# A two-block transformer on one core: the order of the 64x64 F32 products in its two recurrent branches

## The chip, the cores and the metric

The kernel runs on one core of a Trainium2 chip. The time is the device time of one execution in microseconds (us); lower is better. Five engines work side by side, each on its own queue in order: TensorE (PE in the profile; PEld is its weight load, PEq its sequencer), VectorE (DVE), ScalarE (ACT), GpSimdE (POOL) and SyncE (SP), which here only issues transfers. TensorE is an array of 128 by 128 cells. A product whose stationary operand has 64 rows and 64 columns takes one quarter of it: the row half is the half of the 128 partitions that both operands lie on, the column half is the half of the partitions of PSUM, the accumulators, that the result goes to. TensorE's clock has two levels, 2.4 and 1.2 GHz; the profile gives the granted clock as 1.00 and 0.50.

## What is computed

The reference runs 512 tokens of 1024 channels through a first block (differential attention beside a pooling branch, then a mixture of 32 experts) and a second block of two layers. The change lies in the second block. Each of its layers projects the normed input and runs three branches: a gated delta rule (6 heads, "GDN"), latent attention (6 heads, "MLA"), and a second delta rule with its own decays (4 heads, "RWKV"). Both delta rules run over chunks of 64 tokens, forward and backward at once. The part that matters, for the first of them:

```python
def step(s, inp):
    w_c, u0_c, p_c, qg_c, kd_c, ge_c = inp
    u = u0_c - jnp.einsum('nhcd,nhde->nhce', w_c, s)
    o = jnp.einsum('nhcd,nhde->nhce', qg_c, s) + jnp.einsum('nhij,nhje->nhie', p_c, u)
    s = ge_c[..., None, None] * s + jnp.einsum('nhcd,nhce->nhde', kd_c, u)
    return s, o
_, o = lax.scan(step, s0, xs)
```

A head's state `s` is 64x64, and so are the chunk's matrices: every product in a step is 64x64 by 64x64. All is F32.

## The kernel before

Heads come in pairs, one on partitions 0 to 63, the other on 64 to 127 (`par` is the half, `half(i)` its slice). Tokens come in tiles of 128, a tile holding two chunks (`c` is the half). `d` is the direction; at step `st` the forward direction works on chunk `st` and the backward one on chunk `7 - st`, which lie on opposite halves. So `par`, `c` and `d` decide on which quarter of the array a product lies; the pair of heads (`hp` of three in GDN, `cp` of two in RWKV) doesn't.

`Gdn.chain` is the first branch's recurrence. Each of its 8 steps has three blocks of 12 products with vector work between them:
- `kp<-SA,kq`: the state read with k, on all four quarters; VectorE then scales it and subtracts it from v (`rhs`).
- `pu<-rhs,LT`: the chunk's solve, a product with the inverse triangle. Rows and columns are the chunk's half, so only two quarters, the diagonal ones, are used, one for each direction.
- `kp<-VS,KD`: what is added to the state, on all four quarters; VectorE adds it (`SA`). The last step has none.

After the steps come the outputs, for four tiles of tokens: 24 products of the states with q (`kp<-SA,kq`) and 24 of the inner part (`pu<-VS,LT`, diagonal quarters, two directions summed in PSUM), with one buffer each.

`Rwkv.states` has the same shape with 8 products in a block: `kp<-ST,KR`, then `pu<-rhs,LT`, then the state block of 16, where each result is the sum of two products (`kp<-vt,BK` and `kp<-AKV,BK`); then outputs, 16 products `pu<-AKV,RB` and 16 `kp<-ST,KR` a tile. Ahead of it, `products` in `Rwkv.prepare` multiplies a tile's scores with v: 16 products `mm<-vt,SC` on diagonal quarters, for four tiles and two directions.

The order on TensorE is the order in which the program is written. `Net.weave` braids several generators: each yields after some products the time that its next ones wait for other engines, and products of another generator fill that time. GDN's steps are braided with the input projection (`mm<-hh,wh` and its kin, 128x128 by 128x512), RWKV's `prepare` and `states` with MLA and the output projection. These products between two blocks are called fillers below. `Net.matmul` (line 145) issues all products, so they share a line and are told apart by the names of their tiles. The other engines' order is set by the framework's scheduler. An F32 product is recorded as two weight loads and two matmuls, so a block of 12 products shows as 24.

Of the kernel before, what the change touches and what calls it, by code (L numbers as in the profile page):

```python
# [17 lines left out]
S = 512  # L18
# [15 lines left out]
def const_arrays():  # L34
    """Arrays that depend on shapes alone."""
# [32 lines left out]
    # transposed: x -> (-x[16:32], x[0:16]) in each 32  # L68
# [4 lines left out]
    # window / count of the pooling windows that the ends cut  # L73
# [17 lines left out]
def half(p):  # L91
    return slice(64 * p, 64 * p + 64)
# [9 lines left out]

def mm3(net, out, a, b, start, stop):
    """out (+)= a.T @ b for a, b in two float32r parts each."""
    net.matmul(out, a[0], b[0], start=start, stop=False)
    net.matmul(out, a[0], b[1], start=False, stop=False)
    net.matmul(out, a[1], b[0], start=False, stop=stop)


class Net:  # L110
    """What the parts of the kernel share."""

    def __init__(self, ctx, tc, cst, xstack):
# [33 lines left out]
    def warm(self, psum, n):  # L147
        """Products that nobody reads: the tensor engine's clock is halved after an idle time."""
# [57 lines left out]
class Front:  # L206
    """The first block up to its second norm."""

    def __init__(self, net, ctx, ring, a):
# [16 lines left out]
        # normed x, then q and k, then x, by halves of the columns; x after the branch in two float32r parts takes the  # L226
        # place of these and of v and the pooling branch
# [13 lines left out]
    def loads(self, first):  # L241
        """The small inputs: those for the first norm, and the others."""
# [32 lines left out]
    def ada_rows(self, w):  # L275
        """512 columns of silu(c) @ w_ada, as four partial sums, on partitions 0, 32, 64, 96."""
# [10 lines left out]
    def ada_channels(self, i, ws):  # L287
        """mod[i]: a shift and a scale by channel p * 8 + k, and the norm's weight times 1 + scale."""
# [15 lines left out]
    def ada_gates(self):  # L304
        """The gates' rows, on every partition."""
# [22 lines left out]
    def normed(self):  # L328
        """rms_norm(x) by channel, without weights."""
# [16 lines left out]
    def scaled(self):  # L346
        """h = rms_norm(x) * (1 + sc1) + sh1 in two parts."""
# [9 lines left out]
    def in_load(self, i):  # L357
        """Columns 512 i .. of w_in, in halves; the first two lie where the pooling branch and v come later."""
# [10 lines left out]
    def parts(self, w, lo="vector"):  # L369
        """256 columns of w in two parts: a pair by k."""  # L370
# [10 lines left out]
    def by_token(self, i, w, dst, scale=1.0):  # L381
        """Columns 512 i .. of h @ w_in."""
# [10 lines left out]
    def rotary(self, i):  # L393
        """The rotary embedding of the first 16 dims of each component, and channels to partitions."""
# [23 lines left out]
    def pooled(self, w):  # L418
        """The pooling branch, by channel."""
# [38 lines left out]
    def attention(self):  # L458
# [4 lines left out]
        def scores(t, h):  # L463
# [11 lines left out]
            # e0 - lam * (s0 / s1) * e1, for s0 times the weights  # L475
# [35 lines left out]
    def heads(self, t, po, sums):  # L511
        """The normed heads of a tile of tokens, by channel."""
# [24 lines left out]
    def out(self, ws):  # L537
        """x += g1 * (mix @ w_out)."""
# [16 lines left out]
    def router(self):  # L555
        """The router's logits, from x before its norm, and the norm's factors; x in two parts."""
# [3 lines left out]
        # the weights with channels k * 128 + p  # L560
# [63 lines left out]
        # in memory that the parts of x take next: these come first  # L624
# [10 lines left out]
    def out_load(self, i):  # L635
        """Columns 256 i .. of w_out."""
# [58 lines left out]
class Ring:  # L695
    """Tiles of two pools in turn, n[0] of the first, then n[1] of the second."""
# [10 lines left out]
def experts_weights(net, rings, a, pr):  # L707
    """Weights of experts 2 * pr and 2 * pr + 1; pr may be a register."""
# [9 lines left out]
    # by halves of the channels, so that the next ones come as soon as half is done  # L718
# [7 lines left out]
    # by columns for w_down, so that little is left to do after the last  # L726
# [7 lines left out]
class Moe:  # L734
    def __init__(self, net, ctx, rings, a, xd):
# [25 lines left out]
    def route(self):  # L761
# [42 lines left out]
        # 1 + rank, and 0 for the others  # L804
# [15 lines left out]
        # the weights of two experts, and the factor of the norm, in two parts  # L820
# [7 lines left out]
        # the largest rank, for the tokens beyond an expert's first block  # L828
# [9 lines left out]
    def gather(self, rk2, wt2, block=0):  # L838
        """Tokens of ranks block * CAP .. of two experts, by channel; and what their outputs need."""
# [57 lines left out]
    def turned(self, pg, pu):  # L897
        """silu(gate) * up, by channel."""
# [42 lines left out]
    def experts(self, meanwhile):  # L941
        """The first CAP tokens of every expert, by pairs; some other work in between."""
# [27 lines left out]
    def overflow(self):  # L970
        """Experts with more than CAP tokens: the tokens beyond."""
# [26 lines left out]
    def squares(self, t):  # L998
        """x to DRAM; sums for rms_norm(x) * final_g and for the norm after it."""
# [1537 lines left out]
```

## Time and profile before

| | |
|---|---|
| median of three runs | 1983.79 us (1980.91 to 1987.42) |
| span of the profiled execution, first to last instruction | 1989.2 us (no other time of it is given) |
| TensorE matmuls busy | 1766.2 us, 89% of the span |
| VectorE busy | 1064.9 us, 54% |
| ScalarE, GpSimdE busy | 574.7 us, 548.0 us |
| GDN's steps and outputs, first and second layer | from 1038.6 to 1133.5 us and from 1608.9 to 1694.7 us |
| RWKV's states and outputs, first and second layer | from 1289.0 to 1372.4 us and from 1865.6 to 1949.4 us |

Busy time counts a stretch once, however many matmuls are in it, so matmuls that run beside each other on different quarters show as a shorter block and not as a higher share.

### The profile page before, as it was taken

Reading aid. Unit: us, or ns where it says so; the run is one execution under the profiler, and the core shown is the slowest. Engines: PE = TensorE matmul, PEld = TensorE weight load, DVE = VectorE, ACT = ScalarE, POOL = GpSimd, SP = SyncE. Lnnn points to the kernel's source line nnn. Section 1 sums busy time; section 2 is a strip of 40 time slices with the busy share of each in tenths; the row PEclk is TensorE's granted clock in tenths of the full one; section 3 lists DMA queues with packets and bytes.
Section 4 is the critical chain, followed back from the end, with each engine's and each line's share of the span. In section 5 each row is a group of like instructions: output and inputs, shape, how many; then the busy total and the mean of one; then the engine's idle time right before and its main releaser. Section 6 shows DMA issues by size and latency. Waiting matters only on the chain.

```text
span 1989.2 us, 34102 instructions
## 1 busy us (share of the span) xinstructions
PE 1766.2 (89%) x14010; PEld 1207.4 (61%) x14010; DVE 1064.9 (54%) x2260; ACT 574.7 (29%) x1134; POOL 548.0 (28%) x559
## 2 busy tenths in 40 slices
PE   5999998999999999696889988879886989898887
PEld 3985684444444444375677746657674878466566
DVE  2445434434343333568874467636678853756337
ACT  4354432121221212353230144411442220352312
POOL 1122111010101001254621244524356212452433
PEclk7999999999999999898998988869898999795789
DMA  9824628999999999332341201233322511210322
GB/s 312 228 86 149 236 70 320 395 397 394 402 406 394 396 404 373 115 83 70 104 107 48 75 17 27 57 122 109 106 73 59 154 52 61 58 23 15 116 87 81
DMA packets 243218, 337.10 MB, mean 169 GB/s; under 512 B 92768, under 2 KB 166160, under 8 KB 226224
## 3 DMA queue, kind: packets, MB, share of 16 engines
q1 hardware_dynamic: 241152, 329.88, 48.0%
q10 hardware_dynamic: 1152, 3.22, 0.4%
q8 instruction: 112, 1.84, 0.4%
q0 software_dynamic: 752, 1.76, 0.3%
q14 instruction: 50, 0.41, 0.1%
HBM read 310.84 MB, written 23.99 MB: 168 GB/s over the span
## 4 chain that ended last, share of the span: by engine, by line
PE 35%; DVE 13%; DMA 3%; issue 3%; POOL 2%; ACT 2%; SPq 0%; DVEq 0%; POOLq 0%; ACTq 0%
PE mm L145 21%; PE kp L145 4%; PE pu L145 4%; PE mm L155 2%; PE x L145 2%; DVE au L1340 2%; DVE stmp L1338 2%; PE tr L145 1%; DVE M L1561 1%; PE mo L145 1%; DMA w<-in_w_out_dram 1%; PE tr L155 1%; DVE y L1285 1%; DVE wl L1210 1%; POOL w L2311 1%
## 5 line engine op out<-in xcount | busy, mean ns | idle before, releaser
L145 PE MATMUL gu<-w,XT 128*64 128x512 f32 x1024 | 225.8, 594 | 0.0
L145 PE MATMUL mm<-hh,wh 128*128 128x512 f32 (+1 forms) x464 | 201.5, 434 | 1.5 <-DVE rw L1315 1.3
L145 PE MATMUL mm<-hh,wl 128*128 128x512 f32 (+1 forms) x464 | 187.2, 404 | 0.0
L145 PE MATMUL mm<-hl,wh 128*128 128x512 f32 (+1 forms) x464 | 187.0, 403 | 0.0
L924 POOL TENSOR_TENSOR yl<-y,yh 128x512 fp32r<-128x512 f32 x30 | 38.1, 1270 | 451.3 <-ACT yh L923 451.3
L145 PEld LDWEIGHTS gu<-w,XT 128*64 128x64 f32 x1024 | 72.1, 137 | 142.7 <-issue 135.1
L934 DVE TENSOR_TENSOR xres<-mm,xres 128x512 f32<-128x512 f32 x128 | 79.2, 681 | 90.6 <-PE mm L145 90.6
L1208 ACT ACTIVATE wh<-w 128x1024 fp32r<-128x1024 f32 (+1 forms) x54 | 57.0, 1056 | 199.3 <-PE mm L145 135.3
L145 PE MATMUL mm<-w,hT 128*64 128x512 f32 x512 | 113.4, 595 | 0.7 <-ACT hT L908 0.7
L145 PEld LDWEIGHTS mm<-hh,wh 128*128 128x128 f32 (+1 forms) x464 | 90.5, 195 | 27.0 <-issue 5.1
L2239 POOL TENSOR_SCALAR e<-e,rs 128x512 f32<-128x512 f32 x48 | 79.0, 1650 | 97.7 <-DVE rs L2238 85.1
L145 PEld LDWEIGHTS mm<-hh,wl 128*128 128x128 f32 (+1 forms) x464 | 90.6, 195 | 21.0
L145 PEld LDWEIGHTS mm<-hl,wh 128*128 128x128 f32 (+1 forms) x464 | 91.1, 196 | 17.5 <-DVE hl L1156 0.2
L1210 POOL TENSOR_TENSOR wl<-w,wh 128x1024 fp32r<-128x1024 f32 (+1 forms) x28 | 67.6, 2416 | 113.2 <-ACT wh L1208 112.8
L145 PE MATMUL mm<-wh,hh 128*128 128x256 f32 x320 | 94.0, 294 | 2.2 <-ACT hh L353 2.2
L145 PE MATMUL mm<-wh,hl 128*128 128x256 f32 x320 | 91.2, 285 | 4.3 <-DVE hl L355 4.0
L145 PE MATMUL mm<-w,mh 128*128 128x512 f32 x256 | 88.3, 427 | 6.6 <-ACT mh L2362 5.0
L145 PE MATMUL mm<-wl,hh 128*128 128x256 f32 x320 | 90.8, 284 | 1.6 <-DVE wl L377 1.6
L145 PEld LDWEIGHTS mm<-w,hT 128*64 128x64 f32 x512 | 35.3, 137 | 66.7 <-issue 62.0
L1338 DVE TENSOR_TENSOR stmp<-au 96x60 f32<-96x60 f32 (+29 forms) x120 | 62.2, 518 | 16.3 <-DMA au<-rmud 10.5
L922 DVE SCALAR_TENSOR_TENSOR y<-mm,ws,g2b 128x512 f32<-128x512 f32 x32 | 24.0, 751 | 78.2 <-PE mm L145 78.2
L868 ACT ACTIVATE X<-mm,ws 128x512 f32<-128x512 f32 x32 | 22.0, 688 | 151.4 <-DVE ws L865 128.2
(580 smaller groups left out, 3896.6 us busy)
## 6 DMA issues: line engine op xcount, KB each, us to landing
w<-in_w_gate_dram SPq DMA_DIRECT2D x64, 1024.0 KB, 13.1
w<-in_w_up_dram SPq DMA_DIRECT2D x64, 1024.0 KB, 13.7
w<-in_w_down_dram SPq DMA_DIRECT2D x64, 1024.0 KB, 10.1
w<-in_w_in_dram SPq DMA_DIRECT2D x52, 512.0 KB, 4.0
w<-in_w_ada_dram SPq DMA_DIRECT2D x24, 1024.0 KB, 8.4
w<-in_w_out_dram SPq DMA_DIRECT2D x16, 512.0 KB, 4.1
w<-in_w_in_dram SPq DMA_DIRECT2D x6, 1024.0 KB, 11.9
w<-in_w_out_dram SPq DMA_DIRECT2D x4, 1024.0 KB, 6.3
```

The source lines that it names most:

```text
L145: return self.nc.tensor.matmul(out, a, b, **kw)
L155: return self.nc.tensor.transpose(out, a, ident)
L868: nc.scalar.activation(X[:, 512 * i:512 * i + 512], ps, AF.Copy, scale=ws[:, 1:2])
L922: nc.vector.scalar_tensor_tensor(y, py, ws[:, 0:1], net.g2b[:, hs], op0=ALU.mult, op1=ALU.mult)
L924: (nc.vector if last else nc.gpsimd).tensor_tensor(yl[:, hs], y, yh[:, hs].bitcast(F32), op=ALU.subtract)
L934: nc.vector.tensor_tensor(net.xres[:, t, hs], po, net.xres[:, t, hs], op=ALU.add)
L1208: nc.scalar.activation(h[:, :, :m], w[:, :, :m], AF.Copy)
L1210: eng.tensor_tensor(lo[:, :, :m], w[:, :, :m], h[:, :, :m].bitcast(F32), op=ALU.subtract)
L1285: nc.vector.scalar_tensor_tensor(y[:, lo:hi], ps[:, lo + d:hi + d], cw[:, j, m:m + 1], y[:, lo:hi], op0=ALU.mult, op1=ALU.add)
L1338: nc.vector.tensor_tensor(tv, au[:n, :, j + 1:, j:j + 1].to_broadcast(sh), au[:n, :, j:j + 1, 0:j].to_broadcast(sh), op=ALU.mult)
L1340: nc.vector.tensor_tensor(au[:n, :, j + 1:, 0:j], au[:n, :, j + 1:, 0:j], tv, op=ALU.add)
L2239: nc.gpsimd.tensor_scalar(e, e, rs, None, op0=ALU.mult)
```

## The change

Each block's loops are written in another order, so that products that follow each other lie on different quarters. Where four quarters are used, a new table gives their order; where two are, the half alternates. In the state block of RWKV the two products of a sum are pulled apart: first the four of one kind, then the four of the other. The number of products, their operands and what is braided with them are the same. In the outputs of GDN some points where another generator may step in lie elsewhere. Comments are dropped as well, and lines move by up to four (`Net.matmul` is on line 149 now). The pieces shown are the three blocks of a step of `Gdn.chain`, the second half of its outputs, `products` in `Rwkv.prepare`, and the state block of `Rwkv.states`.

```diff
+TURNS = ((0, 0), (1, 1), (0, 1), (1, 0))
...
-                for d in range(2):
-                    for par in range(2):
-                        for hp in range(3):
-                            net.matmul(kp[half(cs[d] % 2), par, hp * 64:hp * 64 + 64], kq[half(par), hp, cs[d], 0:64],
-                                             SA[half(par), st, d, hp], start=True, stop=True)
+                for hp in range(3):
+                    for d, par in TURNS:
+                        net.matmul(kp[half(cs[d] % 2), par, hp * 64:hp * 64 + 64], kq[half(par), hp, cs[d], 0:64],
+                                   SA[half(par), st, d, hp], start=True, stop=True)
...
-                for d in range(2):
-                    h = half(cs[d] % 2)
-                    for u in range(6):
+                for u in range(6):
+                    for d in range(2):
+                        h = half(cs[d] % 2)
...
-                    for d in range(2):
-                        h = half(cs[d] % 2)
-                        for par in range(2):
-                            for hp in range(3):
+                    for hp in range(3):
+                        for d, par in TURNS:
+                            h = half(cs[d] % 2)
...
-                for c in range(2):
-                    for u in range(6):
-                        for d in range(2):
+                for u in range(6):
+                    for d in range(2):
+                        for c in range(2):
...
-                    for c in range(2):
-                        for u in range(4):
-                            h = 2 * (u % 2) + u // 2
-                            for j in range(2):
+                    for u in range(4):
+                        h = 2 * (u % 2) + u // 2
+                        for j in range(2):
+                            for c in range(2):
...
-                for d in range(2):
-                    h = half(cs[d] % 2)
-                    t = cs[d] // 2
-                    for par in range(2):
-                        for cp in range(2):
+                for cp in range(2):
+                    for i in (1, 0):
+                        for d, par in TURNS:
+                            h, t = half(cs[d] % 2), cs[d] // 2
                             out = pS[half(par), d, cp * 64:cp * 64 + 64]
                             hs = slice((2 * cp + par) * 64, (2 * cp + par) * 64 + 64)
-                            net.matmul(out, BK[h, t, d, 1, hs], vt[h, t, hs], start=True, stop=False)
-                            net.matmul(out, BK[h, t, d, 0, hs], SS[h, st, par * 2 + cp], start=False, stop=True)
+                            net.matmul(out, BK[h, t, d, i, hs], vt[h, t, hs] if i else SS[h, st, par * 2 + cp],
+                                       start=(i == 1), stop=(i == 0))
```

The other two blocks of RWKV's steps and the outputs' blocks of both branches are reordered in the same way. TensorE's order shows it where the names of neighbours differ. The first state block of RWKV, ahead of the change, where the two kinds follow each other eight times:

```order
L145 MATMUL mo<-t_11778,vt 64x128
L145 MATMUL kp<-vt,BK 64x64
L145 MATMUL kp<-AKV,BK 64x64
...
L145 MATMUL kp<-AKV,BK 64x64
L155 MATMUL mm<-cst,e 128x128 x4
L145 MATMUL mo<-t_11785,vt 64x128
```

The same place after it:

```order
L149 MATMUL mo<-t_11778,vt 64x128
L149 MATMUL kp<-vt,BK 64x64 x4
L149 MATMUL kp<-AKV,BK 64x64 x4
L149 MATMUL kp<-vt,BK 64x64 x4
L149 MATMUL kp<-AKV,BK 64x64 x4
L159 MATMUL mm<-cst,e 128x128 x4
L149 MATMUL mo<-t_11785,vt 64x128
```

The 16 products stand between the same neighbours, now in four turns of four quarters. The outputs of RWKV, first layer, TensorE before, from the last solve on:

```order
L145 MATMUL pu<-rhs,LT 64x64 x8
L145 MATMUL pu<-AKV,RB 64x64 x8
L145 MATMUL kp<-ST,KR 64x64 x8
...
L145 MATMUL pu<-AKV,RB 64x64 x8
L145 MATMUL kp<-ST,KR 64x64 x8
```

And after:

```order
L149 MATMUL pu<-rhs,LT 64x64 x8
L149 MATMUL pu<-AKV,RB 64x64 x16
L149 MATMUL kp<-ST,KR 64x64 x16
L149 MATMUL pu<-AKV,RB 64x64 x16
L149 MATMUL kp<-ST,KR 64x64 x16
```

A tile's two halves were done one after the other and are done in turns now. In all other blocks the names read the same before and after; only the halves within them change places.

## Rows read from the trace of the kernel before

**Rows 1.** The page: the span, and busy time of each engine.

```profile
span 1989.2 us, 34102 instructions
PE 1766.2 (89%) x14010; PEld 1207.4 (61%) x14010; DVE 1064.9 (54%) x2260; ACT 574.7 (29%) x1134; POOL 548.0 (28%) x559
```

**Rows 2.** Stretches: length, busy PE, PEld, DVE, ACT, POOL (count), clock, DMA share, GB/s.

```profile
1087.00:1117.00 30.00, 30.00 (x319) 23.18 (x319) 10.29 (x17) 2.76 (x5) 7.31 (x10) 1.00 0.11 41
1118.00:1133.40 15.40, 15.40 (x385) 15.37 (x383) 6.63 (x15) 0.00 (x0) 6.51 (x7) 1.00 0.15 46
1323.00:1357.00 34.00, 34.00 (x334) 25.84 (x333) 12.61 (x25) 3.61 (x6) 6.50 (x10) 0.87 0.15 51
```

**Rows 3.** The chain of waits: start us, length us, what.

```profile
1090.94 1.36 PE pu L145 x24
1092.30 1.58 PE mm L145 x6
1093.88 1.00 PE kp L145 x24
...
1323.87 2.86 PE mm L145 x6
```

**Rows 4.** Timeline of PE: start, length, line, operation, tiles, count [idle before <-releaser].

```profile
918.21 0.74 PE L145 MATMUL x<-kq 64*64 64x64 f32 x24
...
1293.56 0.33 PE L145 MATMUL kp<-vt,BK 64*64 64x64 f32 x2
1293.72 0.28 PE L145 MATMUL kp<-AKV,BK 64*64 64x64 f32 x2
1293.84 0.33 PE L145 MATMUL kp<-vt,BK 64*64 64x64 f32 x4
...
1294.82 0.28 PE L145 MATMUL kp<-AKV,BK 64*64 64x64 f32 x2
...
1297.45 0.48 PE L145 MATMUL kp<-ST,KR 64*64 64x64 f32 x16
...
1301.99 0.73 PE L145 MATMUL kp<-ST,KR 64*64 64x64 f32 x16 [0.58 <-DVE ST L2068]
```

**Rows 5.** Timeline of PE: blocks that the change reorders, and two waits.

```profile
1045.39 2.42 PE L145 MATMUL pu<-rhs,LT 64*64 64x64 f32 x24 [3.22 <-DVE rq L1695]
...
1050.82 1.72 PE L145 MATMUL kp<-VS,KD 64*64 64x64 f32 x24
...
1090.87 1.43 PE L145 MATMUL pu<-rhs,LT 64*64 64x64 f32 x24
...
1093.81 1.07 PE L145 MATMUL kp<-VS,KD 64*64 64x64 f32 x24
...
1234.88 3.31 PE L145 MATMUL mm<-vt,SC 64*64 64x64 f32 x32 [5.57 <-DVE SC L1945]
...
1247.25 1.90 PE L145 MATMUL mm<-vt,SC 64*64 64x64 f32 x32
...
1317.42 0.73 PE L145 MATMUL kp<-ST,KR 64*64 64x64 f32 x16 [2.87 <-DVE ST L2068]
...
1349.05 0.96 PE L145 MATMUL pu<-rhs,LT 64*64 64x64 f32 x16
```

**Rows 6.** Timeline of DVE and POOL in a tile of the first branch's outputs.

```profile
1119.63 0.56 DVE L1715 TENSOR_TENSOR KD<-kp,gam 128x384 f32<-128x384 f32 x1 [1.01 <-PE kp L145]
...
1120.73 1.04 POOL L1728 TENSOR_TENSOR KD<-KD,rhs 128x384 f32<-128x384 f32 x1 [11.34 <-DVE rhs L1715]
...
1122.14 0.56 DVE L1729 TENSOR_TENSOR KD<-KD,pu 128x384 f32<-128x384 f32 x1 [1.22 <-PE pu L145]
```

**Rows 7.** The second branch's outputs: chain of waits, then a row of DVE's timeline.

```profile
1358.09 1.14 PE pu L145 x16
...
1361.31 1.08 PE pu L145 x16
...
1360.78 0.42 DVE L2091 TENSOR_TENSOR YK<-pu,YK 128x256 f32<-128x256 f32 x1 [2.74 <-PE pu L145]
```

More of the change, by code (lines that the diff above doesn't have):

```diff
@@ L1704, in chain @@
                 pqv = pq[:, :, :384].rearrange("p a (z h d) -> p z a h d", z=2, h=3)
-                for c in range(2):
-                    ch = 2 * t + c
+                for hp in range(3):
                     for d in range(2):
-                        st = ch if d == 0 else 7 - ch
-                        for par in range(2):
-                            for hp in range(3):
-                                net.matmul(pqv[half(c), d, par, hp], kq[half(par), hp, ch, 64:128], SA[half(par), st, d, hp],
-                                           start=True, stop=True)
-                        yield 0
+                        for c, par in TURNS:
+                            ch = 2 * t + c
+                            st = ch if d == 0 else 7 - ch
+                            net.matmul(pqv[half(c), d, par, hp], kq[half(par), hp, ch, 64:128], SA[half(par), st, d, hp],
+                                       start=True, stop=True)
+                    yield 0
                 for d in range(2):
@@ L1951, in products @@
                     pv = psum.tile([128, 512], F32, name="mm", bufs=2)
-                    for c in range(2):
-                        for u in range(4):
-                            h = 2 * (u % 2) + u // 2
-                            for j in range(2):
+                    for u in range(4):
+                        h = 2 * (u % 2) + u // 2
+                        for j in range(2):
+                            for c in range(2):
                                 net.matmul(pv[half(c), 256 * j + u * 64:256 * j + u * 64 + 64], SU[half(c), u, 64 * j:64 * j + 64],
-                                                 vt[half(c), t, h * 64:h * 64 + 64], start=True, stop=True)
+                                           vt[half(c), t, h * 64:h * 64 + 64], start=True, stop=True)
                     pvv = pv.rearrange("p (x u k) -> p x u k", x=2, u=4)
@@ L2036, in states @@
                 ks = psum.tile([128, 2, 512], F32, name="kp", bufs=1)
-                for d in range(2):
-                    for par in range(2):
-                        for cp in range(2):
-                            net.matmul(ks[half(cs[d] % 2), par, cp * 64:cp * 64 + 64], KR[half(par), d, cp, cs[d], 0:64],
-                                             ST[half(par), st, d, cp], start=True, stop=True)
+                for cp in range(2):
+                    for d, par in TURNS:
+                        net.matmul(ks[half(cs[d] % 2), par, cp * 64:cp * 64 + 64], KR[half(par), d, cp, cs[d], 0:64],
+                                   ST[half(par), st, d, cp], start=True, stop=True)
                 rh = tmp.tile([128, 4, 64], F32, name="rhs")
@@ L2046, in states @@
                 pu = psum.tile([128, 512], F32, name="pu", bufs=1)
-                for d in range(2):
-                    h = half(cs[d] % 2)
-                    for u in range(4):
+                for u in range(4):
+                    for d in range(2):
+                        h = half(cs[d] % 2)
                         net.matmul(pu[h, u * 64:u * 64 + 64], LTu[h, d, cs[d] // 2, u], rh[h, u], start=True, stop=True)
@@ L2078, in states @@
                 pr = psum.tile([128, 2, 512], F32, name="kp", bufs=1)
-                for c in range(2):
-                    for u in range(4):
-                        for d in range(2):
-                            st = 2 * t + c if d == 0 else 7 - 2 * t - c
-                            net.matmul(po[half(c), u * 64:u * 64 + 64], RBu[half(c), d, t, u], SS[half(c), st, u],
-                                             start=(d == 0), stop=(d == 1))
-                    for par in range(2):
-                        for cp in range(2):
-                            for d in range(2):
-                                st = 2 * t + c if d == 0 else 7 - 2 * t - c
-                                net.matmul(pr[half(c), par, cp * 64:cp * 64 + 64], KR[half(par), d, cp, 2 * t + c, 64:128],
-                                                 ST[half(par), st, d, cp], start=(d == 0), stop=(d == 1))
+                step = lambda c, d: 2 * t + c if d == 0 else 7 - 2 * t - c
+                for u in range(4):
+                    for d in range(2):
+                        for c in range(2):
+                            net.matmul(po[half(c), u * 64:u * 64 + 64], RBu[half(c), d, t, u], SS[half(c), step(c, d), u],
+                                       start=(d == 0), stop=(d == 1))
+                for cp in range(2):
+                    for d in range(2):
+                        for c, par in TURNS:
+                            net.matmul(pr[half(c), par, cp * 64:cp * 64 + 64], KR[half(par), d, cp, 2 * t + c, 64:128],
+                                       ST[half(par), step(c, d), d, cp], start=(d == 0), stop=(d == 1))
                 nc.vector.tensor_tensor(YK[:, t], po[:, :256].rearrange("p (u k) -> p u k", u=4), YK[:, t], op=ALU.add)
```

17 lines of the change are left out of this document (7 added, 10 removed).

## The prediction

> **What bounds the kernel now.** I read the page first, then the busy time by stretches, the chain of waits, and the timeline of single engines around each block that the change reorders. The page [rows 1] says only that TensorE (PE) is busy for 89% of a span of 1989.2 us. The stretches say where: from 1087 to 1117 us, inside the first branch's steps, PE is busy for 30.00 of 30.00 us at full clock while VectorE (DVE) works 10.29; over the branch's outputs it is busy for 15.40 of 15.40; in the second branch's steps for 34.00 of 34.00 [rows 2]. The chain of waits runs through PE there without a break: a `pu` block, six projection products, a `kp` block [rows 3], more products. Whoever shortens a block there moves all that follows. The vector work between two blocks is covered by those fillers, and they stay as they are.
>
> **How long a block takes, and why.** A 64x64 F32 product shows as two matmuls. In the block that adds to the state, a queue of one quarter reads as follows: two matmuls start 0.16 us before the next pair, later pairs 0.12 apart [rows 4]; so the second starts 0.107 us after the first, each later one 0.058 after the one before, and the last lasts 0.22. N matmuls on one quarter thus take 0.107 + 0.058(N-2) + 0.22 us. The `kp<-ST,KR` block, 16 matmuls in runs of four per quarter, lasts 0.48 us [rows 4]: exactly N = 4 (0.44) plus 0.04 between the first and the last quarter's start. So four quarters can run at full pace side by side, and 0.04 is the price of starting them. At half clock the same block lasts 0.73 [rows 4]; an estimate that fits it is a step of 0.107 there, a first one of 0.16 and an end of 0.31: 0.16 + 0.107(N-2) + 0.31, and 0.04 for four queues.
>
> Longer runs don't get this. The `kp<-VS,KD` block has runs of six on each of four quarters and takes 1.07 us [rows 5]; with four full queues of six it would be 0.60. In the state block the second queue's first product starts at 1293.84 with the fifth matmul of the first queue (`x4` begins there): the engine looks about three waiting matmuls ahead on a quarter, and a run of eight holds up the other quarters until five have started. The third witness is `x<-kq`: the same 24 matmuls of the same shape, written with neighbours on two quarters, last 0.74 [rows 4].
>
> **The change part by part.** No instruction is added or removed; PE's order changes only inside blocks, and the fillers between blocks stay where they are. DVE, ScalarE, SyncE swap some neighbours elsewhere; I cost that at nothing, with 2 us either way. By the formula, per block at full clock (half clock in brackets):
> - `pu` of the first branch: two queues of 12, 0.91 against 1.43 [rows 5]: -0.52 (1.55 against 2.42: -0.87).
> - `kp` of the first branch, both kinds: four queues of six, 0.60 against 1.07: -0.47 (0.94 against 1.72: -0.78) [rows 5].
> - `pu` of the second: two queues of 8, 0.68 against 0.96 [rows 5]: -0.28 (-0.48).
> - its state block: four queues of 8 make 0.71; it lasts 1.54 now (1293.56 to 1295.10, [rows 4]): -0.83 (-1.4).
> - `mm<-vt,SC`: two queues of 16, 1.14 against 1.90: -0.76 (1.98 against 3.31: -1.33) [rows 5].
> - `kp<-ST,KR` in the steps: already balanced, 0.
>
> The lower bound of each gain is no gain, if neighbours conflict in a way that these rows don't show; the upper bound is the formula, and for `kp` the weakest witness is `x<-kq`, 0.33 instead of 0.47. I take the formula, since `kp<-ST,KR` is the same kind of block with all four quarters.
>
> *First branch, steps.* 16 `pu` (three at half clock, one partly), 14 `kp` that add to the state (two at half clock), 16 that read it. Three of the last lie ahead of a wait for DVE, the longest 3.22 us [rows 5], and give nothing. 12 x 0.52 + 3 x 0.87 + 0.75 + 12 x 0.47 + 2 x 0.78 + 13 x 0.47 = **22.9 us**.
>
> *First branch, outputs.* Four tiles of 128 tokens a layer, 15.40 us [rows 2], so 3.85 a tile. PE would need 12 + 24 places in the queues, 36 x 0.058 = 2.1 us. But now DVE and GpSimdE (POOL) are late next: two DVE scalings 0.56 each, overlapped to about 1.1, a POOL sum of 1.04, the DVE sum of 0.56 [rows 6], about 2.6 us with the hand-overs, and `pu` has one buffer that this last sum frees. First tile 2.2, three more at 2.6, and the last product's end: about 10.4 instead of 15.4: -5.0 a layer, **10.0**.
>
> *Second branch, steps.* Steps 1 and 2 of each layer give nothing: PE then stands 2.87 us ahead of step 3 for DVE's addition [rows 5], which is queued behind loads. What step 0 gains passes on, since the loads are issued behind an output product that follows it. Left are nine `pu` at full clock and three at half, seven state blocks and three: 9 x 0.28 + 3 x 0.48 + 7 x 0.83 + 3 x 1.4 = **14.0**.
>
> *Second branch, outputs.* A tile takes 3.2 us (1358.09 to 1361.31, [rows 7]), and DVE stands idle 2.74 us for it. PE would need 16 + 8 places, 1.5 us; DVE's five instructions a tile, 0.42 or less each, make 1.9 to 2.1 with hand-overs and pace it. Four tiles at 1.9: 12.8 - 7.6 = 5.2 a layer, **10.4**.
>
> *Products of the scores with v.* 16 blocks, 12 at full clock. About half stand ahead of a wait for DVE or ScalarE and are worth nothing; the one at 1234.88 had itself waited 5.57 us for DVE [rows 5], which does the triangular solve there. Eight are in stretches where PE runs on, four of these at half clock: 4 x 0.76 + 4 x 1.33 = 8.4. As DVE is late too there, I take half, **4**.
>
> Sum: 22.9 + 10.0 + 14.0 + 10.4 + 4 = 61.3 us. The profiled span is 1989.2, so 1927.9; the median of the runs shown, 1983.79, is 5.4 lower, and 61.3 off it gives **1922.5 us**.
>
> **The rivals.**
> (a) *One PSUM bank at a time.* `pu`, `mm<-vt,SC` and the outputs' `pu` put both diagonal quarters into one bank. If two could not write a bank together, only the blocks that spread over banks would gain: 13.3 in the first branch's steps, some 0.6 x 8 = 5 in its outputs, 10.0 from state blocks, some 7.5 in the second's outputs, 36 in all, **1948**. Against it: 24 matmuls of `pu` one after the other would last 0.107 + 22 x 0.058 + 0.22 = 1.60, and last 1.43; 32 of `mm<-vt,SC` would last 2.07, and last 1.90 [rows 5]. So the end of one queue and the start of the other already overlap in one bank. The Trainium skill ("TensorEngine Tiling (Array Packing)", Gotcha 1: PSUM Pressure) states this rule: different row tiles cannot access the same bank at the same time. By it the time would be that of this rival; the trace disagrees with it where the row tiles write different partitions of the bank.
> (b) *The gain is swallowed by the others.* If DVE and POOL already paced the outputs, the solve all the products, and the loads the start of the second branch, 10.0 + 10.4 + 4 + 3 would go: 34 left, **1950**. For it: the waits for DVE in [rows 5]. Against: in both outputs DVE's idle time ends with PE, 1.22 and 2.74 us [rows 6, 7].
> (c) *Slower: the clock.* Where PE's blocks shrink and waits appear, the granted clock may fall to its half level. Six fillers then last 2.86 instead of 1.58 [rows 3]; a step with three fillers costs 3 x 1.28 and some 1.3 for its blocks, 5.1 us. Twelve more steps of the 32 at half clock would eat the gain, twenty give **2025**. Against: the steady steps run without idle time [rows 2], and shorter blocks leave none between them.
> (d) *No change.* If the engine's look-ahead already did this reordering, the time stays at **1984**. Against: 1.07 for runs of six, 0.74 for alternating neighbours of the same size.
>
> **How the numbers follow.** Forecast 0.78, with its own range 1906 (no loss in the outputs, all products count) to 1940 (`kp` at the weaker witness, products nothing, a few waits); (a) 0.06, (b) 0.10, (c) 0.03, (d) 0.03. The range 1906 to 1949 leaves out the ends of (b), (c) and (d). A difference under 0.3%, 6 us, is about what a measurement of this kernel can't tell from none. Faster: 0.78 + 0.06 + 0.10 = 0.94; same 0.03; slower 0.03.
>
> **What the profile after would show.** Right: `pu` x24 at 0.91, `kp` x24 at 0.60, the state block at 0.71 and `mm<-vt,SC` x32 at 1.14 us at full clock; the span from the first branch's first output to its last about 10.4; PE's busy total some 70 us lower, and its idle time in front of outputs ended by DVE. Wrong: blocks as long as before (d), only `pu` and `vt,SC` as long (a), blocks short but idle time in their place (b), more stretches at half clock in the steps (c).

## The result and the profile after

The changed kernel takes 1930.22 us (median of four runs, 1927.28 to 1931.57), the kernel before 1984.65 beside it: ratio 0.9724 [0.9686, 0.9761], 54.4 us less. Forecast were 1922.5 with 1906 to 1949, so the direction, the range and the mechanism held; 61.3 us were forecast. The two profiled executions differ by 59.4 us. One later execution of the changed kernel took 2037.00 us at a mean granted clock of 0.80, where all others told of here have 0.90 to 0.92, and no time or ratio here counts it. The page of the kernel after, for [rows 1]:

```profile
span 1929.8 us, 34104 instructions
PE 1675.8 (87%) x14010; PEld 1119.3 (58%) x14010; DVE 1062.8 (55%) x2260; ACT 573.9 (30%) x1134; POOL 548.8 (28%) x559
```

As many matmuls, 90 us less of busy time, where some 70 were forecast. Some 20 of the 90 are chance of one execution: the second executions of both kernels (below) have 1744.4 and 1672.3, which is 72 less. The stretches that answer to [rows 2] (first branch's steps, its outputs, second branch's steps; columns as there):

```profile
1080.00:1108.00 28.00, 27.68 (x366) 20.11 (x366) 10.41 (x18) 2.74 (x4) 7.51 (x10) 1.00 0.22 77
1110.00:1120.80 10.80, 9.51 (x395) 8.89 (x391) 6.81 (x15) 0.11 (x1) 6.17 (x7) 1.00 0.21 65
1306.00:1340.60 34.60, 31.25 (x369) 22.14 (x369) 14.79 (x30) 4.92 (x8) 11.71 (x15) 0.86 0.19 63
```

PE now stands for 1, 12 and 10% of these stretches, where it never stood; the outputs of a layer fit in 10.8 us instead of 15.4. The blocks, from PE's timeline of the kernel after, beside [rows 4, 5]:

```profile
1080.38 0.92 PE L149 MATMUL pu<-rhs,LT 64*64 64x64 f32 x24
...
1082.80 0.58 PE L149 MATMUL kp<-VS,KD 64*64 64x64 f32 x24
...
1319.44 0.68 PE L149 MATMUL pu<-rhs,LT 64*64 64x64 f32 x16
...
1321.64 0.34 PE L149 MATMUL kp<-vt,BK 64*64 64x64 f32 x8
...
1322.04 0.30 PE L149 MATMUL kp<-AKV,BK 64*64 64x64 f32 x8
...
1323.85 0.46 PE L149 MATMUL kp<-ST,KR 64*64 64x64 f32 x16
...
1718.37 1.15 PE L149 MATMUL mm<-vt,SC 64*64 64x64 f32 x32
```

Every block has the length of the formula: 0.92 for 0.91, 0.58 for 0.60, 0.68, the state block 0.70 (1321.64 to 1322.34) for 0.71, 1.15 for 1.14. So rival (d) is out, and so is (a): `pu` and `mm<-vt,SC` write one bank from two quarters and gain like the others.

Where the time went, stage by stage, on PE's timeline: chains and states from their first product to the last of their outputs, the other stages between them, the last one to the end of the last instruction on DVE. "Again" is a second execution of each kernel on a later occasion (below):

| us | before | after | before again | after again | forecast |
|---|---|---|---|---|---|
| start to the first branch's chain | 1038.6 | 1040.7 | 1038.9 | 1041.3 | 0 |
| chain with outputs, layer 1 | 94.9 | 80.1 | 94.6 | 80.3 | -16.5 |
| preparation of the second branch | 155.5 | 157.2 | 154.5 | 157.1 | -2 |
| its states with outputs | 83.4 | 73.7 | 80.7 | 72.1 | -12.2 |
| to the next chain | 236.5 | 237.4 | 236.4 | 236.0 | 0 |
| chain with outputs, layer 2 | 85.8 | 71.7 | 85.8 | 74.2 | -16.4 |
| preparation | 171.0 | 155.9 | 158.6 | 154.8 | -2 |
| states with outputs | 83.7 | 71.3 | 82.1 | 70.1 | -12.2 |
| to the end of the work | 36.6 | 38.5 | 36.6 | 39.0 | 0 |

The outputs' new pace, first branch, DVE and POOL in one tile of the kernel after, for [rows 6]:

```profile
1113.86 0.55 DVE L1716 TENSOR_TENSOR KD<-kp,gam 128x384 f32<-128x384 f32 x1
1114.33 0.55 DVE L1716 TENSOR_TENSOR rhs<-kp,gam 128x384 f32<-128x384 f32 x1
1115.99 0.55 DVE L1729 TENSOR_TENSOR KD<-KD,pu 128x384 f32<-128x384 f32 x1 [1.11 <-POOL KD L1728]
...
1114.96 1.00 POOL L1728 TENSOR_TENSOR KD<-KD,rhs 128x384 f32<-128x384 f32 x1
```

DVE's idle time, which PE ended before, is now ended by POOL's sum; the tiles' `pu` blocks start at 1111.36, 1114.00, 1116.60 and 1119.20, the 2.6 us of the forecast. The second branch's outputs, PE's last two tiles, then DVE and POOL, for [rows 7]:

```profile
1345.89 1.09 PE L149 MATMUL pu<-AKV,RB 64*64 64x64 f32 x30 [1.44 <-DVE YK L2088]
...
1350.09 1.09 PE L149 MATMUL pu<-AKV,RB 64*64 64x64 f32 x30 [1.00 <-DVE YK L2088]
...
1344.88 0.56 DVE L2358 SCALAR_TENSOR_TENSOR y<-mix,gate 128x384 f32<-128x384 f32 x1 [1.11 <-POOL ml L2360]
...
1346.99 1.88 DVE L2094 TENSOR_SCALAR mean<-mean 128x4 f32<-128x4 f32 x1
...
1339.20 4.69 POOL L2308 TENSOR_TENSOR w<-w,w 128x1024 fp32r<-128x1024 f32 x2 [3.09 <-ACT w L2306]
...
1346.47 2.38 POOL L2308 TENSOR_TENSOR w<-w,w 128x1024 fp32r<-128x1024 f32 x1 [1.63 <-ACT w L2306]
```

PE waits for DVE, and DVE in two ways for POOL, which splits output weights there (2.4 us each): the instruction at 1344.88 needs a POOL result that stands behind two of them, and the scaling of 128x4 numbers at 1346.99, 0.16 us elsewhere, lasts until POOL's subtraction ends. From the first tile's start to the last one's pass 8.9 us (layer 2: 10.3) and not 5.7. The kernel before had this already in one tile of four, in both layers; its DVE and POOL in the second tile:

```profile
1366.09 2.53 DVE L2098 TENSOR_TENSOR y<-y,mean 128x256 f32<-128x256 f32 x1
...
1365.98 2.35 POOL L2311 TENSOR_TENSOR w<-w,w 128x1024 fp32r<-128x1024 f32 x1
```

PE stood nowhere in those outputs, so it cost nothing.

### The profile page after: what moved, and what is told of

It is laid out like the page before. It is cut to its first block, busy times and chain, and to the rows that moved or that the text cites. A ratio compares the mean times of both kernels' runs of the same rounds, so it can differ in the third digit from the quotient of the medians.

```text
span 1929.8 us, 34104 instructions
## 1 busy us (share of the span) xinstructions
PE 1675.8 (87%) x14010; PEld 1119.3 (58%) x14010; DVE 1062.8 (55%) x2260; ACT 573.9 (30%) x1134; POOL 548.8 (28%) x559
## 3 DMA queue, kind: packets, MB, share of 16 engines
q10 hardware_dynamic: 1152, 3.22, 0.5%
## 4 chain that ended last, share of the span: by engine, by line
PE 26%; DVE 16%; issue 5%; DMA 4%; POOL 3%; ACT 2%; SPq 0%; DVEq 0%; POOLq 0%; ACTq 0%
PE mm L149 18%; DVE au L1344 2%; PE mm L159 2%; DVE stmp L1342 2%; PE x L149 2%; PE tr L149 1%; PE pu L149 1%; PE kp L149 1%; DVE M L1565 1%; POOL w L2308 1%; DMA w<-in_w_out_dram 1%; DVE wl L1214 1%; PE tr L159 1%; DVE y L1289 1%; PE mo L149 1%
## 5 line engine op out<-in xcount | busy, mean ns | idle before, releaser
L149 PEld LDWEIGHTS gu<-w,XT 128*64 128x64 f32 x1024 | 72.1, 137 | 142.7 <-issue 135.6
L149 PEld LDWEIGHTS mm<-hl,wh 128*128 128x128 f32 (+1 forms) x464 | 91.6, 197 | 17.5 <-DVE hl L1160 0.2
```

The lines of the kernel that those rows point to most:

```text
L149: return self.nc.tensor.matmul(out, a, b, **kw)
```

## The experiments

**Parts of the change.** Four kernels on one chip; each takes some functions from before and some from after, as the expectations say, so that their diffs are pieces of the one shown above.

> Only the first branch's chain is reordered (its `pu`, both kinds of `kp`, its outputs); the second branch's blocks and the products of the scores with v stand as before. My theory, that each block is worth what its longest queue loses: the steps of both layers give 20 to 23 us and the outputs 9 to 10, so 29 to 33 us, ratio 0.983 to 0.986; `pu` x24 lasts 0.91 us and `kp` x24 0.58 to 0.60 at full clock, the second branch's state block still 1.54. Rival, that the blocks' gain is made up by waits or by clock in later stages: under 20 us, ratio above 0.990.

> Only the second branch's steps and outputs are reordered. My theory: steps 14 to 16 us, outputs by the prediction 10.4, by the trace of the changed kernel 6 (PE is seen to wait 1.0 to 2.4 us for DVE ahead of the later tiles); so 20 to 26 us, ratio 0.987 to 0.990, nearer 20. Rival, that the 15.1 us which the changed kernel gains in the second layer's preparation of this branch come with this edit: 35 us, ratio 0.982.

> Only the products of the scores with v (`mm<-vt,SC`) are reordered. The prediction: 4 us, ratio 0.998. Its rival: the blocks shorten to 1.14 us and the wait for DVE that follows grows by as much, 0 us, ratio 1.000. A third reading: these blocks carry the 15.1 us of the second layer's preparation, ratio 0.992.

> The whole change except the products of the scores with v, which stand as before. The prediction: 4 us slower than the changed kernel, so about 50 us faster than before, ratio 0.975. If these products are hidden behind DVE: as fast as the changed kernel, ratio 0.9725. If they carry the second layer's preparation: ratio 0.980.

| | median | ratio to before (1977.59) |
|---|---|---|
| first branch only | 1962.30 | 0.9930 [0.9909, 0.9952] |
| second branch only | 1960.78 | 0.9915 [0.9884, 0.9946] |
| products only | 1981.61 | 1.0021 [0.9998, 1.0044] |
| all but the products | 1939.86 | 0.9804 [0.9771, 0.9838] |

The stages that were edited gain about what the theory says: the chain lasts 79.9 and 72.0 us in the first kernel, the states 72.6 and 69.2 in the second. Yet the first kernel gains 15 us in all where its chains gain 28, the products alone bring nothing (4 us more, the interval reaches to none), and in company they seem worth 10 or more: 0.9804 without them, 0.9724 with them. In the first and the third my theory's total fails and the rival's holds (under 20 us and a ratio above 0.990; no gain); the second gains 16.8 us, where 20 to 26 were expected, and 20 lies inside its interval. What differs outside the edited stages is above all the preparation: in its second layer 164.1, 163.6 and 166.5 us in the three of these kernels without reordered products, 154.9 in the one with them. No TensorE order was touched there but the products', and DVE's row of instructions had moved: the triangular solve is a chain of 60 DVE instructions, and the masks of the scores (`SC`, L1945), for which the products wait, are interleaved with it by the scheduler. In some kernels the third group of masks stands behind 42 or 43 of the 60 ("early"), in others behind 53 or more ("late"). In the kernel before both layers are early; in the changed one the first is late, the second early; with the first branch alone, or all but the products, both are late.

**The changed kernel again**, without any edit, in a later session:

> The changed kernel once more, beside the others on one chip, as the measure for them and for the kernel without the reordered products, whose ratio was 0.980. If those products are worth 10 us or more in company, as the stage times of the second layer say (155 to 156 us with them, 164 to 171 without): ratio 0.972 to 0.975. If they are worth 4 us or less: 0.978 to 0.980.

1929.90 us, ratio 0.9743 [0.9701, 0.9785]: the gain repeats. Beside the 1939.86 us of the kernel without these products they are worth some 10 us in company, though the intervals of the two ratios overlap a little.

**DVE's row or the products' blocks?** Two mirror images that part the two, by one condition (the first is shown, the second has `self.l == 0`):

```diff
-for u in range(4):
-    h = 2 * (u % 2) + u // 2
-    for j in range(2):
-        for c in range(2):
+turned = [(c, u, j) for u in range(4) for j in range(2) for c in range(2)]
+for c, u, j in turned if self.l == 1 else sorted(turned):
+            h = 2 * (u % 2) + u // 2
```

> The changed kernel with the products of the scores with v reordered in the second layer only. DVE's row of instructions inside the triangular solve of the preparation then takes three groups of score masks into the solve in neither layer: the third stands at its very end, in both layers, as in the kernel with all but the products. Theory A, DVE's order sets the length of the preparation and the products' own blocks nothing: the second layer's preparation lasts 162 to 167 us as there, although its blocks are short (1.15 us), and the ratio is 0.980. Theory B, the shorter blocks are what counts: 155 to 156 us as in the changed kernel, ratio 0.974.

> The mirror image: the products reordered in the first layer only. DVE's row is word for word that of the changed kernel in both solves (the third group of masks early in the second layer), while the second layer's blocks last 1.90 us again. Theory A (DVE's order): the second layer's preparation lasts 155 to 157 us, ratio 0.974. Theory B (shorter blocks): 163 to 167 us, ratio 0.980.

The first measured 1942.74 us, 0.9806 [0.9769, 0.9844], the second 1937.03, 0.9769 [0.973, 0.9808]; the second layer's preparation 160.3 (short blocks, late masks) and 157.9 us (long blocks, early masks). Two of its products on PE's timeline with the late row, in the first of these kernels, and the third group of masks on DVE's, with seven of the solve's 60 instructions behind it:

```profile
1769.65 1.98 PE L149 MATMUL mm<-vt,SC 64*64 64x64 f32 x32 [4.45 <-DVE SC L1945]
...
1783.08 1.97 PE L149 MATMUL mm<-vt,SC 64*64 64x64 f32 x32 [1.87 <-DVE SC L1945]
...
1790.93 0.73 DVE L1945 TENSOR_TENSOR SC<-x,mk 128x256 f32<-128x256 f32 x2
```

and with the changed kernel's early row, 18 of the 60 behind the masks:

```profile
1763.55 1.97 PE L149 MATMUL mm<-vt,SC 64*64 64x64 f32 x32 [2.86 <-DVE SC L1945]
...
1775.05 1.76 PE L149 MATMUL mm<-vt,SC 64*64 64x64 f32 x32
...
1780.24 0.75 DVE L1945 TENSOR_TENSOR SC<-x,mk 128x256 f32<-128x256 f32 x2
```

In the changed kernel's second execution the first of these waits is longer:

```profile
1765.18 1.97 PE L149 MATMUL mm<-vt,SC 64*64 64x64 f32 x32 [5.46 <-DVE SC L1945]
```

Neither theory is right alone, and the sizes are rough. Against the changed kernel's second layer (155.9 and 154.8 us) the late row with the same short blocks costs 4.4 to 5.5 us, the long blocks with the same row 2.0 to 3.1. Over the second layer of the kernels told of here, the preparation lasts 155 us with early masks and short blocks (154.8 to 155.9, three profiles; 148.5 in a fourth, told of below, whose third group stands behind 38 of the 60), 158 with early and long (157.9, 158.6; one disturbed stretch of the first profile left out, below), 160 with late and short (158.1 to 162.1, four), 165 with late and long (163.6 to 166.5, three): about 5 us or more for the row and 3 to 5 for the blocks. In the first layer it is 150.8 to 158.6 us with early masks (seven profiles, mean 155.0) and 156.2 to 163.8 with late ones (seven, mean 159.2).

Part of these differences is TensorE's clock, which no run here holds still. The mean granted clock of these stages lies between 0.79 and 0.89, and two of the three second layers with late masks and long blocks (163.6, 166.5) have 0.81, while the third (164.1) has 0.86 and those with early and long ones have 0.86 and 0.87. The first layer of the second mirror image has the blocks of the changed kernel and its masks in the same places, and lasts 160.1 us at 0.85 against 157.2 and 157.1 at 0.87, so 3 us can come without either cause. For short blocks the row's part also shows in what PE waits for masks in the second layer, 7.0 to 11.7 us in the late rows and 2.6 to 5.5 in the early ones; for long blocks it doesn't (3.4 to 7.4 against 5.8 to 7.0), and there the row's part is only argued. In the totals of the two mirror images the intervals overlap.

**The kernel before again.**

> The kernel before once more, for a second profile, whose second layer's preparation took 171 us in the first, 44 of half clock in one stretch among them. If that stretch was chance of that execution: 158 to 164 us and a span near 1976. If it belongs to the kernel: 169 to 172 and a span near 1985. The first branch's chain should repeat 94.7 and 86 to 88 us, the second's states 82 to 84.

1973.12 us, span 1971.4, preparation 158.6. Here is the stretch of the solve in the first profile, then in this one:

```profile
1791.00:1838.00 47.00, 40.14 (x272) 29.16 (x272) 30.70 (x93) 11.83 (x28) 11.20 (x8) 0.56 0.02 5
```

```profile
1787.00:1834.00 47.00, 37.23 (x340) 25.32 (x338) 39.30 (x110) 18.33 (x42) 17.35 (x12) 0.85 0.13 32
```

A granted clock of 0.56 against 0.85. So 12.4 of the 15.1 us in that row of the table were chance of one execution. Executions of the kernel before spread from 1967.87 to 1986.45 us beside the four parts above, and from 1973.75 to 1994.59 on the same chip later.

**How far TensorE looks ahead.** Runs of two products on a quarter (`kp` of the first branch, and the state block and `pu` of the second) or three (`pu` of the first) in place of one; three of these edits:

```diff
-for hp in range(3):
-    for d, par in TURNS:
+for hp, d, par in [(hp, d, par) for hps in ((0, 1), (2,)) for d, par in TURNS for hp in hps]:
...
-for u in range(6):
-    for d in range(2):
+for u, d in [(u, d) for us in ((0, 1, 2), (3, 4, 5)) for d in range(2) for u in us]:
...
-for i in (1, 0):
-    for d, par in TURNS:
+for d, par in TURNS:
+    for i in (1, 0):
```

> The changed kernel with longer runs on a quarter: in the first branch's steps `kp` goes in runs of two products (four matmuls) per quarter, `pu` in runs of three products (six matmuls); in the second branch's steps the state block and `pu` go in runs of two products (four matmuls). My theory, three matmuls waiting on a quarter: a run of four holds nobody up, so `kp` x24 stays at 0.58 to 0.60, the state block x32 at 0.70 to 0.72 and `pu` x16 at 0.68 to 0.70 us at full clock; a run of six holds the other quarter until its third matmul starts, 0.107 + 0.058 = 0.165 us, so `pu` x24 lasts 0.91 + 0.16 = 1.07. Rival, neighbours must lie on different quarters: `kp` over 0.8, the state block over 1.0 and `pu` x24 about 1.2 (halfway to the 1.43 of runs of twelve).

```profile
1087.20 1.08 PE L149 MATMUL pu<-rhs,LT 64*64 64x64 f32 x24 [0.32 <-DVE rhs L1661]
...
1089.82 0.60 PE L149 MATMUL kp<-VS,KD 64*64 64x64 f32 x24
...
1323.53 0.36 PE L149 MATMUL kp<-vt,BK 64*64 64x64 f32 x8
...
1323.98 0.30 PE L149 MATMUL kp<-AKV,BK 64*64 64x64 f32 x7
...
1328.11 0.73 PE L149 MATMUL pu<-rhs,LT 64*64 64x64 f32 x16
```

Runs of six matmuls cost the forecast 0.16 us; runs of four cost 0.02 to 0.06 (0.60, 0.73, state block 0.75), a little more than the expected nothing. The rival, that neighbours must alternate, is out. The same three waiting matmuls give the blocks of the kernel before too: a run of N holds the next quarter until its (N-3)th matmul starts. By the prediction's steps that makes 0.91 + 0.51 = 1.42 us for `pu` x24 in runs of twelve (1.43 in [rows 5]), 1.14 + 0.75 = 1.89 for `mm<-vt,SC` in runs of sixteen (1.90), 0.68 + 0.28 = 0.96 for `pu` x16 in runs of eight (0.96), 0.56 + 3 x 0.165 = 1.05 for `kp` x24 in runs of six (1.07). An execution took 1939.28 us.

**The other engines in the outputs.**

```diff
-nc.gpsimd.tensor_tensor(ov, ov, t2, op=ALU.add)
-nc.vector.tensor_tensor(o, o, po[:, :384].rearrange("p (u d) -> p u d", u=6), op=ALU.add)
+tv = t2.rearrange("p a h d -> p (a h) d")
+nc.vector.tensor_tensor(tv, tv, po[:, :384].rearrange("p (u d) -> p u d", u=6), op=ALU.add)
+nc.gpsimd.tensor_tensor(ov, ov, t2, op=ALU.add)
...
-nc.vector.tensor_scalar(mean[:, ms], mean[:, ms], 1.0 / 64, None, op0=ALU.mult)
-nc.vector.tensor_tensor(y[:, t], y[:, t], mean[:, ms, None].to_broadcast([128, 4, 64]), op=ALU.subtract)
+nc.vector.scalar_tensor_tensor(y[:, t], mean[:, ms, None].to_broadcast([128, 4, 64]), -1.0 / 64, y[:, t],
+                               op0=ALU.mult, op1=ALU.add)
```

> The changed kernel with two edits on the other engines in the outputs. First branch: DVE adds `pu` to the second scaled tile itself and POOL adds the two afterwards, so that DVE waits for no POOL sum. Second branch: the mean's tiny scaling on DVE and the subtraction are one instruction. My theory: the first branch's outputs are paced by the hand-over DVE, POOL, DVE, 2.60 us a tile, and go to about 2.2, PE's own 2.1 (1.2 us a layer); in the second branch the tiny scaling, which takes 0.16 us and took 1.88 and 0.89 beside POOL's subtraction, is gone, and 1.5 to 2.5 us a layer with it; together 5 to 7 us below the changed kernel. Rival: another DVE instruction is stretched beside POOL in its place, then 2 to 3 us in all; if PE paced the first branch's outputs, nothing there.

1926.51 us, 0.9705 [0.9663, 0.9746], 3.4 us below the changed kernel's median on the same chip, with intervals that overlap; 5 to 7 were expected. First branch: DVE waits for PE again:

```profile
1111.72 0.56 DVE L1729 TENSOR_TENSOR rhs<-rhs,pu 128x384 f32<-128x384 f32 x1 [0.42 <-PE pu L149]
```

In the first layer the first three tiles start 2.27 us apart; the fourth comes 3.17 later, with 0.68 us of PE's time put down to issue. From the first tile's start to the last one's 0.1 us is gained there and 0.6 to 0.9 in the second layer (8.1 for 8.6 and 9.0 in the two profiles), where 1.2 were expected. Second branch: the rival was right. The fused instruction is stretched in the scaling's place, to 0.3 us behind the end of POOL's:

```profile
1336.08 2.03 DVE L2095 SCALAR_TENSOR_TENSOR y<-mean,y 128x256 f32<-128x256 f32 x1
...
1335.45 2.37 POOL L2309 TENSOR_TENSOR w<-w,w 128x1024 fp32r<-128x1024 f32 x1 [1.65 <-ACT w L2307]
```

First to last tile still take 8.4 and 8.2 us. So the same two instructions went to ScalarE, with the first branch's edit kept and the products reordered in the second layer alone, which makes both layers' masks early:

```diff
+nc.scalar.activation(mean[:, ms], mean[:, ms], AF.Copy, scale=-1.0 / 64)
+for h in range(4):
+    nc.scalar.activation(y[:, t, h], y[:, t, h], AF.Identity, bias=mean[:, 4 * t + h:4 * t + h + 1])
```

> The changed kernel with the first branch's outputs edit as before, the mean's scaling and subtraction of the second branch's outputs on ScalarE instead of DVE, and the products reordered in the second layer only, which with these edits gives DVE rows that have all three groups of score masks early in the solve in both layers. Theory: the stretching of DVE beside POOL concerns instructions that read two operands from SBUF (or the tiny scaling), so what is left on DVE in the outputs (sums with PSUM, a reduction) keeps 0.42 us, and the second branch's outputs lose the 1.5 us waits that follow a stretched instruction: first to last tile 6.5 to 7.0 us against 8.9 and 10.3; rival: DVE's remaining instructions or ScalarE's are stretched too, 8.2 to 8.5 as with the fused instruction. Preparation 151 to 155 us in both layers; in all 8 to 14 us below the changed kernel, ratio 0.967 to 0.970.

```profile
1347.59 0.42 DVE L2088 TENSOR_TENSOR YK<-pu,YK 128x256 f32<-128x256 f32 x1 [0.27 <-PE pu L149]
1348.12 0.42 DVE L2089 TENSOR_TENSOR y<-kp,YK 128x256 f32<-128x256 f32 x1
1348.58 0.42 DVE L2093 TENSOR_REDUCE mean<-y 128x4 f32<-128x256 f32 x1
...
1346.93 2.39 POOL L2309 TENSOR_TENSOR w<-w,w 128x1024 fp32r<-128x1024 f32 x1 [1.52 <-DVE y L2089]
```

Sums with PSUM and the reduction keep 0.42 us beside POOL, and PE's wait ahead of the last tile is gone; the wait for POOL's queued result (1.39 us) stays, so the tiles take 7.8 us, not 6.5 to 7.0. The second layer's preparation falls to 148.5 us, the first's stays at 157.0, and from the states to the next layer 122.1 us pass where 116 to 118 did in other kernels here; in all 1930.65 us, 0.9754 [0.9715, 0.9793], no gain. That last stage ends at the next layer's first `x<-kq`; over its first 122 us the granted clock is 0.87, in both profiles of the changed kernel 0.92. The clock explains part of what it grew by; why it fell there was not followed up.

**The blocks that the change left out**, on top of the outputs' edits: `x<-kq` and `x<-KR,BB` in turns.

> As the kernel with the two edits in the outputs, and with neighbours on different quarters in the 64x64 blocks that the change left out: `x<-kq` of the first branch, `x<-KR,BB` of the second. The formula: `x<-kq` x24 from 0.74 to 0.58 us, the block of products ahead of the scores from 1.28 to about 0.95. If all counted, 16 x 0.16 + 16 x 0.33 = 7.9 us; those ahead of waits for DVE count nothing, and I take 3 to 4. So 8 to 11 us below the changed kernel with the outputs' edits, ratio to the kernel before about 0.967. Rival: all of these blocks are hidden behind DVE, no difference to the kernel with the outputs' edits alone.

The blocks shorten as computed (`x<-kq` 0.578 us, the one ahead of the scores 0.90), and the time is 1925.79 us, 0.9701 [0.9664, 0.9739]: no difference to the kernel with the outputs' edits alone. That is the rival's total; its reason, that DVE covers these blocks, isn't shown, since between the two profiled executions the chain's start lies 8.7 us later (5.9 of them ahead of the first shortened block) and the chain of the first layer is 3.7 shorter.

## Why the prediction was right, and where it was off

- *How long a block takes, and why.* Right to 0.02 us in every block, at full clock and at half (`pu` x24 1.54 for 1.55, `mm<-vt,SC` 1.97 for 1.98). The witness was the balanced block in [rows 4], and the queue read off its neighbour. The runs of six show that the look-ahead of about three, read there, predicts a new order too, and the blocks of the kernel before agree with it.
- *First branch, steps and outputs*: forecast 22.9 + 10.0; the chains gave 28.9 in the first pair of profiles and 25.9 in the second. The outputs gave 4.8 and 4.1 us a layer, then 4.7 and 3.7, for 5.0: 2.6 us a tile as forecast, but the second layer's last tile comes 3.3 us behind the third. The steps gave 20.0 and 17.5. The prediction has the vector work between two blocks covered by the fillers; that is not quite so. Over the steps of both layers PE stood 5.9 us before and stands 9.5 and 10.1 after, mostly for DVE (the 3.22 us ahead of the first block of [rows 5] became 3.99). That covers what is missing in the first pair and most of it in the second, whose second layer also has 3.4 us more at half clock.
- *Second branch*: forecast 14.0 + 10.4 = 24.4; measured 22.1 and 20.6. The outputs are the mis-sized term: 3.8 and 2.4 us a layer, then 3.8 and 2.6, and not 5.2. "Five instructions a tile, 0.42 or less each" is the misreading: in the kernel before the subtraction took 2.53 us in one tile of four, beside POOL's weight subtraction, where PE was still slower than DVE. With PE faster, more of DVE's instructions fall beside these subtractions and are stretched or queued behind them. The first outputs edit and the ScalarE edit show both waits. The steps gave 16.0 and 14.2 for 14.0, with some luck: 5.9 and 4.8 in the first layer, but 10.1 and 9.4 in the second, where the granted clock also rose, from 0.71 to 0.79 and from 0.75 to 0.78.
- *Products of the scores with v*: 4 forecast. Their blocks are worth some 2 to 5 us in the second layer, and little that could be told from chance in the first.
- "*DVE, ScalarE, SyncE swap some neighbours elsewhere; I cost that at nothing, with 2 us either way*" is the step that failed. The first layer's preparation, forecast 2 us shorter, is 1.7 and 2.6 longer with its late masks; the end takes 1.9 and 2.4 more, and 0.4 to 3.4 more in every other kernel run; the chain starts 2.1 and 2.4 later. That is 8 to 9 us of the forecast. For the preparation the runs show that the row has a part, and that the clock of one execution can move it by 3 us. For the end the row is only argued, and for the chain's start the cause stays open: the delay is there at the first layer's first `x<-kq` (918.2 became 920.4, again 917.9 and 921.0), before any product of the change has run, and in the other kernels with a reordered chain it lies anywhere from 1036.9 to 1045.6.
- Rival (b), swallowed gain, was partly true, in the second branch's outputs and for the products. Rival (c) was not: the mean granted clock is 0.912 after and 0.909 before, and over several executions on one chip 0.910 to 0.916 after and 0.904 to 0.918 before, though where half clock falls in one execution moves a stage by more than 10 us.
- *The sum was made against its own time.* The 5.4 us between that execution and the median were taken off; that was right, and the second profile says in which stage that execution lost them.
- *That the total came so near is partly luck.* The second pair of profiles, without that stretch, is 43.2 us apart, 18 less than the sum: 7.0 are missing in the first branch, 3.8 in the second, 4.6 in the first layer's preparation and 2.4 each at the chain's start and at the end, while two other stages give 2.2 back. The medians are 54.4 apart, and 50.1 in the later session; that execution of the kernel before lies 8.8 us below the median of the others beside it.

## What to carry to other kernels

Issue 64x64 F32 products so that at most four matmuls in a row lie on one quarter of the array, and read from one block that is balanced already what the others would take. Then ask what paces the stage once TensorE is faster, and price the other engines' instructions with what they will then stand beside: look for the slowest record of each, not the usual one. And where a scheduler orders the other engines, compare their rows before and after as well, and the granted clock of the stage: a swap in a row that nobody edited seems worth some 5 us here, and one stretch mostly at half clock 12.

## What the runs showed of the hardware

- A quarter holds about three waiting matmuls (64x64, F32): runs of six on two quarters lengthen a block by 0.16 us (1.08 against 0.92), runs of twelve by 0.51 (1.43), runs of four by 0.02 to 0.06.
- Two quarters on a diagonal write one PSUM tile (`pu`, 512 F32 a partition; the bank of rival (a)) at full pace: 24 matmuls in 0.92 us, where one after the other would take 1.60 by the prediction's steps.
- A DVE instruction that starts beside a running POOL subtraction of weights ends 0.3 us behind it if it reads two operands of 128x256 from SBUF (0.42 became 2.03, and 2.53 in the kernel before), 0.03 behind it if it is the scaling of 128x4 from SBUF (0.16 became 1.88); with one operand from PSUM, or as a reduction, it keeps 0.42. The Trainium skill ("SBUF — State Buffer", Who interferes with whom) says this: DVE and GpSimd share a port pair that one of them holds for a whole instruction, a DVE instruction with two SBUF inputs contends with a GpSimd one that reads SBUF, a `tensor_scalar` can in its 2-port modes, and one with at most one SBUF input outside these modes doesn't. The traces agree.
